# Token halves of the projections inside the k-tile loop: wh·xh0, wh·xl0, wh·xl1, wh·xh1, wl·xh1, wl·xh0

## The chip, the cores and the metric

The kernel runs on one core of a Trainium2 chip. The metric is the device time of one execution in microseconds (us), the median over several runs. The core has five engines that run beside each other, each through its own instructions in order: PE (TensorE, the matmuls, with PEld for its weight loads), DVE (VectorE), ACT (ScalarE), POOL (GpSimd) and SP (which issues DMAs here). They wait for each other by semaphores.

## The reference, cut to what matters

One layer of a decoder with two groups of heads side by side, 16 heads of stick-breaking attention ("sb") and 16 of sliding-window attention ("sw", 4 key and value heads), for 1024 tokens and a model width of 2048, in float32:

```python
h = rmsnorm(x, norm_pre)
proj = h @ w_in                    # (1024, 2048) @ (2048, 6656)
q_sb, k_sb, v_sb, z_sb, q_sw, k_sw, v_sw, z_sw = split(proj)
o_sb = stick_breaking_attention(q_sb, k_sb, v_sb)
o_sw = sliding_window_gqa(q_sw, k_sw, v_sw, sinks, rel_bias)
# each group: rmsnorm with its gain, times silu of its gate z
y = concat(gated o_sb, gated o_sw) @ w_out
out = x + rmsnorm(y, norm_post)
```

The change is in `h @ w_in`. The kernel computes it transposed: 52 row blocks of 128 output channels, each 128 x 1024 tokens.

## The kernel before

**The work.** x and the weights are each split into a high and a low part (xh and xl, whi and wlo), and a product is the sum of three matmuls: whi·xh, whi·xl and wlo·xh. From 0 to 76.7 us, x is loaded and split while three row blocks are computed. From 76.7 to about 1500 us the other 49 row blocks follow in the order of the list `work` (L727 to L735), one call of `proj` each. From 1500 us on comes the output projection (L909).

**One projection.** `proj` takes two PSUM tiles from `pproj` (L82), one for each half of the tokens (half 0 and half 1, 512 columns each). The tag has three buffers, and they rotate: half 0 of the next projection gets the buffer that is longest free, and half 1 of the next projection gets the buffer that half 0 of this one used. The depth of 2048 is 16 k-tiles of 128, in four weight groups `kg` of four. For each group `split_w` (L128) loads the weights, ACT makes whi (L133) and DVE makes wlo (L135); the split of the group after it is called at the head of each group. Within a group, the four k-tiles of half 0 come first, then those of half 1, three matmuls of 128 x 512 each: 96 matmuls for a projection.

**What is inserted.** After every three matmuls, `step()` (L252) may insert one piece of the attention, by a count of the PE time that the matmuls so far stand for: four matmuls z (the scores; then ACT's sigmoids L532 and L534, two scans on DVE L545 or L542, and a product L548), up to four transposes (wt, L126; then ACT's copy L563 and DVE's difference L564), or four matmuls o. Matmuls and transposes stay in program order on PE (L122, L126). The order of the other engines' instructions is set by a scheduler when the program is built.

**After a projection.** `proj` returns, and `done(ps)` in the main loop evacuates it: `scaled` (L362) multiplies a PSUM half with the row scale rstd on DVE (L366, 128 x 512, out of PSUM into a tile u), half 0 first. `evac_qk` splits and stores the result, `evac_v` transposes it, and `evac_z` gates the attention output with it (sigmoid L417, products L418 and L424). A half's PSUM buffer is free once L366 has read it.

Of the kernel before, what the change touches and what calls it, by code (L numbers as in the profile page):

```python
# [22 lines left out]
KT = D // P  # L23
HALF = 512
# [33 lines left out]
def layer(ctx, tc, xT, x, w_first, w_blk, w_out, g_pre, g_post, g_sb, g_sw, sinks, rel, onehot, penalty, out):  # L58
# [23 lines left out]
    def pproj(name):  # L82
        return ptile("pp", name, 3)
# [33 lines left out]
    def mm(ps, a, b, start, stop):  # L117
        n = 1
        for d in b.shape[1:]:
            n *= d  # L120
        pe_time[0] += n / 2400.0 * (4 if n < 256 or b.dtype == F32 else 1)
        tc.keep_in_program_order(nc.tensor.matmul(ps, a, b, start=start, stop=stop))  # L122
# [5 lines left out]
    def split_w(name, src):  # L128
        n = src.shape[1]
        raw = wr.tile([P, n, P], F32, tag="wraw", name=f"wraw_{name}", bufs=3)  # L130
        nc.sync.dma_start(raw, src)
        hi = wr.tile([P, n, P], F32R, tag="whi", name=f"whi_{name}")
        nc.scalar.copy(hi, raw)  # L133
        lo = wr.tile([P, n, P], F32R, tag="wlo", name=f"wlo_{name}")
        nc.vector.tensor_sub(lo, raw, hi.bitcast(F32))  # L135
        return hi, lo
# [15 lines left out]
    def advance(force=False):  # L152
        now = pe_time[0]
        while waiting and (force or waiting[0][0] <= now):
            todo.extend(waiting.pop(0)[1])
            prep()
        if later and (force or later[0][0] <= now):
            later.pop(0)[1]()
            return True
        if stage2 and (force or stage2[0][0] + stage2[0][1]["lag2"] <= now):  # L160
            u = stage2.pop(0)[1]
            u["s3"]()
            left[u["key"]] -= 1
            return True
        if stage1 and len(stage2) < 3 and (force or stage1[0][0] + stage1[0][1]["lag"] <= now):
            u = stage1.pop(0)[1]
            u["s2"]()
            stage2.append((pe_time[0], u))
            return True
        if todo and len(stage1) < todo[0]["depth"] and (force or last_start[0] + todo[0]["period"] <= now):  # L170
            u = todo.pop(0)
            if not u["ready"]:
                u["prep"]()
            last_start[0] = max(last_start[0] + u["period"], now - u["period"])
            u["s1"]()
            stage1.append((pe_time[0], u))
            prep()
            return True
        return False
# [10 lines left out]
    def background(force=False):  # L190
        for ch in chains:
            while force or pe_time[0] >= ch["at"]:
                if ch["job"] is None:
                    if not jobs:
                        break
                    ch["job"] = jobs.pop(0)(ch["buf"])
                wait = next(ch["job"], None)
                if wait is None:
                    ch["job"] = None
                else:  # L200
                    ch["at"] = pe_time[0] + wait
# [50 lines left out]
    def step():  # L252
        advance()
        background()
# [12 lines left out]
    xh, xl, xraw = [], [], []  # L267
# [73 lines left out]
    for k in range(KT):  # L341
# [11 lines left out]
        wh, wl = first.pop(0)  # L353
        parts = [(b, h) for h in range(2) for b in range(len(FIRST))]
        for b, h in sorted(parts) if k == KT - 1 else parts:
            for i, (wt, xt) in enumerate(((wh, xh[k]), (wh, xl[k]), (wl, xh[k]))):
                mm(ps0[b][h], wt[:, b, :], xt[:, h * HALF:(h + 1) * HALF],
                   start=(k == 0 and i == 0), stop=(k == KT - 1 and i == 2))
# [91 lines left out]
    def proj(b, name, nxt=None, mid=None):  # L450
        def get(b, name, kg):
            return split_w(f"{name}_{kg}", w_blk[b, :, 4 * kg:4 * kg + 4, :])

        if not splits:
            splits.append(get(b, name, 0))
        ps = [pproj(f"p_{name}_{h}") for h in range(2)]
        for kg in range(4):
            wh, wl = splits.pop(0)
            if kg == 2 and mid is not None:
                mid()  # L460
            if kg < 3:
                splits.append(get(b, name, kg + 1))
            elif nxt is not None:
                splits.append(get(*nxt, 0))
            for h in range(2):
                for j in range(4):
                    k = 4 * kg + j
                    for i, (wt, xt) in enumerate(((wh, xh[k]), (wh, xl[k]), (wl, xh[k]))):
                        mm(ps[h], wt[:, j, :], xt[:, h * HALF:(h + 1) * HALF],
                           start=(k == 0 and i == 0), stop=(k == KT - 1 and i == 2))  # L470
                    step()
        return ps

    kk = []
# [351 lines left out]
    for n, (b, name, done) in enumerate(work):  # L826
        nxt = work[n + 1][:2] if n + 1 < len(work) else None
        if DBG:
            print(name, f"{pe_time[0]:.0f}", {k: v for k, v in left.items() if v})
        ps = proj(b, name, nxt, mids.get(name))  # L830
        if n == len(work) - 3:
            drain(f"sb{NPAIR - 1}")
        if nxt is None:
            split_wo(2)
        done(ps)
        if n == len(work) - 3:
            open_ph2()
# [9 lines left out]
    def bank(name):  # L847
        tg = PT2[next(slots) % 8]
        return ptile(tg, name, PB[tg])
# [63 lines left out]
    for i in range(LAST + 1):  # L913
        nxt, src = [], []
        for dc in range(2):
            k0 = (2 * i + dc) * 8
            if i == LAST and dc == 1:
                split_wo(k0 + 8)
                for tb in range(4):
                    for h in range(1 + (tb == 3)):  # L920
                        part = slice(h * 256, (h + 1) * 256) if tb == 3 else whole
                        ps = bank(f"y{i}_{dc}_{tb}_{h}")[:, :part.stop - part.start]
# [8 lines left out]
            for e in range(8):  # L931
# [16 lines left out]
                if i == 5:  # L948
                    n = dc * 8 + e
                    residual("2", *pieces[n], scales[pieces[n][0]], x_rows[n])  # L950
                    load_row(n + 2)
                if i == LAST and dc == 0:
                    tb, h = divmod(e, 2)
# [58 lines left out]
```

## Time and profile before

| | |
|---|---|
| time, median of 3 runs | 1822.48 us (1818.33 to 1823.29) |
| profiled execution | 1825.41 us, its span 1823.7 us |
| busy share of PE, PEld, DVE, ACT, POOL | 98%, 82%, 68%, 43%, 27% |
| matmuls on record (weight loads as many) | 9046 |
| longest wait of PE after the first 20 us | 2.4 us (y for wohl, L775) |
| mean granted clock | 0.996 |

PE is the time in which a matmul is on the array, and PEld that of the weight loads beside it. The stretches named in the prediction are counted from the start of the span. Names in a row read out<-in: p_ is a projection's PSUM tile (its matmuls), u_ the evacuated half, whi_ and wlo_ the weight parts, z_, m_, b_, wt_, wh_, wl_ and o_ the tiles of an attention unit, in that order.

### The profile page before, as it was taken

The page shows a single profiled execution, that of the slowest core. Times are in us where ns is not written, and L with a number is a line of the kernel's source. Part 1 is how long each engine was busy: PE and PEld are TensorE (multiplying, and loading weights), DVE is VectorE, ACT ScalarE, POOL GpSimd, SP SyncE. Part 2 cuts the span into 40 slices and gives each one's busy share as a digit, 9 for nine tenths or more (in the row PEclk, how much of TensorE's full clock was granted, in tenths as well). Part 3 has the DMA queues.
Part 4 walks back from the last instruction along what each step waited for, and adds up shares of the span by engine and source line. Part 5 has one row for each costly group of instructions (what it writes and reads, how often), then busy time and mean ns, then how long its engine had stood idle before and what let it go on. Part 6 is the DMA issues. An engine that isn't in the chain of part 4 may idle for free. (4 is left out here: it accounts for less than half of the span.)

```text
span 1823.7 us, 27416 instructions
## 1 busy us (share of the span) xinstructions
PE 1786.3 (98%) x9046; PEld 1493.2 (82%) x9046; DVE 1242.3 (68%) x1984; ACT 787.2 (43%) x1696; POOL 496.2 (27%) x648
## 2 busy tenths in 40 slices
PE   8999999999999999999999999999999999999997
PEld 7788778887888888888888888888888877888886
DVE  7558842588557688587676787767868546745876
ACT  7345531355334344343443444434434434445432
POOL 0011121111213234133232332223303214504523
PEclk9999999999999999999999999999999999999999
DMA  7547775576746656466556563454524376533485
GB/s 229 193 143 206 197 202 167 163 205 199 217 145 191 179 159 199 138 191 173 174 163 181 159 183 124 135 176 127 175 76 132 116 227 211 189 107 128 145 248 184
DMA packets 205421, 312.50 MB, mean 171 GB/s; under 512 B 26176, under 2 KB 85728, under 8 KB 205152
## 3 DMA queue, kind: packets, MB, share of 16 engines
q1 hardware_dynamic: 203216, 307.61, 56.1%
q10 hardware_dynamic: 2064, 3.15, 0.5%
q8 instruction: 72, 1.18, 0.3%
q14 instruction: 69, 0.57, 0.1%
HBM read 219.42 MB, written 91.23 MB: 170 GB/s over the span
## 5 line engine op out<-in xcount | busy, mean ns | idle before, releaser
L545 DVE TENSOR_TENSOR_SCAN m_sb<-m_sb,m_sb,zero 128x257 f32<-128x257 f32 x192 | 159.9, 871 | 49.9 <-ACT m_sb L532 46.8
L548 DVE TENSOR_TENSOR b_sb<-b_sb,m_sb 128x512 f32<-128x512 f32 x160 | 128.3, 802 | 25.2 <-POOL b_sb L538 13.8
L532 ACT ACTIVATE m_sb<-z_sb 128x512 f32<-128x512 f32 x160 | 95.9, 600 | 114.4 <-PE z_sb L122 101.6
L542 DVE TENSOR_TENSOR_SCAN m_sb<-m_sb,mask 128x256 f32<-128x256 f32 x128 | 119.0, 967 | 38.6 <-ACT m_sb L532 36.9
L909 PE MATMUL y<-wohi,x 128*128 128x512 f32 x448 | 140.7, 390 | 0.5 <-ACT wohi L774 0.5
L563 ACT CAST wh_sb<-wt_sb 128x512 fp32r<-128x512 f32 (+1 forms) x160 | 87.0, 544 | 116.3 <-PE wt_sb L126 115.9
L909 PE MATMUL y<-wohl,x 128*128 128x512 f32 x576 | 134.4, 393 | 2.4 <-DVE wohl L775 2.4
L564 DVE TENSOR_TENSOR wl_sb<-wt_sb,wh_sb 128x512 fp32r<-128x512 f32 (+1 forms) x160 | 100.5, 631 | 45.4 <-ACT wh_sb L563 44.6
L909 PEld LDWEIGHTS y<-wohl,x 128*128 128x128 f32 x576 | 109.2, 190 | 25.7 <-DVE wohl L775 2.9
L122 PE MATMUL p_zsb<-xh,whi_zsb 128*128 128x512 f32 x256 | 103.9, 406 | 1.6 <-ACT whi_zsb L133 1.4
L122 PE MATMUL p_zsw<-xh,whi_zsw 128*128 128x512 f32 x256 | 104.8, 409 | 0.0
L122 PE MATMUL p_qsb<-xh,whi_qsb 128*128 128x512 f32 x256 | 104.5, 408 | 0.0
L122 PE MATMUL p_ksb<-xh,whi_ksb 128*128 128x512 f32 x256 | 104.4, 408 | 0.0
L122 PE MATMUL p_vsb<-xh,whi_vsb 128*128 128x512 f32 x256 | 102.9, 402 | 0.0
L122 PE MATMUL p_zsb<-xh,wlo_zsb 128*128 128x512 f32 x256 | 101.4, 396 | 1.3 <-DVE wlo_zsb L135 1.3
L122 PE MATMUL p_zsw<-xh,wlo_zsw 128*128 128x512 f32 x256 | 101.4, 396 | 0.0
L122 PE MATMUL p_zsw<-xl,whi_zsw 128*128 128x512 f32 x256 | 101.1, 395 | 0.0
L122 PE MATMUL p_ksb<-xh,wlo_ksb 128*128 128x512 f32 x256 | 101.1, 395 | 0.0
L122 PE MATMUL p_zsb<-xl,whi_zsb 128*128 128x512 f32 x256 | 101.1, 395 | 0.0
L122 PE MATMUL p_qsb<-xh,wlo_qsb 128*128 128x512 f32 x256 | 100.8, 394 | 0.0
L122 PE MATMUL p_ksb<-xl,whi_ksb 128*128 128x512 f32 x256 | 100.8, 394 | 0.0
L122 PE MATMUL p_vsb<-xh,wlo_vsb 128*128 128x512 f32 x256 | 100.6, 393 | 0.0
(242 smaller groups left out, 4926.7 us busy)
## 6 DMA issues: line engine op xcount, KB each, us to landing
row_sw<-in_w_out SPq DMA_DIRECT2D x80, 256.0 KB, 4.3
bg<-in_w_out SPq DMA_DIRECT2D x80, 256.0 KB, 4.2
woraw<-wsum SPq DMA_DIRECT2D x80, 256.0 KB, 3.4
kh<-kd SPq DMA_DIRECT2D x160, 64.0 KB, 3.0
kl<-kd SPq DMA_DIRECT2D x160, 64.0 KB, 2.8
wsum<-row_sw SPq DMA_DIRECT2D x40, 256.0 KB, 2.6
wsum<-bg SPq DMA_DIRECT2D x40, 256.0 KB, 2.8
q_sw<-qd SPq DMA_DIRECT2D x64, 128.0 KB, 3.4
```

The costliest lines, as they stand in the source:

```text
L122: tc.keep_in_program_order(nc.tensor.matmul(ps, a, b, start=start, stop=stop))
L532: nc.scalar.activation(m[:, :, 1:257], z, AF.Sigmoid, scale=-SCALE)
L542: nc.vector.tensor_tensor_scan(m[:, tb, 1:257], m[:, tb, 1:257], mask[:, P - P * tb:P - P * tb + 256], m[:, tb, 0:1], ALU.mult, ALU.max)
L545: nc.vector.tensor_tensor_scan(m[:, tb, :], m[:, tb, :], zero.to_broadcast([P, 257]), prev[:, tb, 256:257], ALU.mult, ALU.max)
L548: nc.vector.tensor_mul(beta, beta, m[:, :, 0:256])
L563: nc.scalar.copy(wh[:, :k], pt[:, :k])
L564: nc.vector.tensor_sub(wl[:, :k], pt[:, :k], wh[:, :k].bitcast(F32))
L909: nc.tensor.matmul(ps, xt[:, a, tcols], w[b][:, cols], start=first and n == 0, stop=last and n == 2)
```

## The change

The loop over the four k-tiles of a group becomes the outer one, and each k-tile takes its six matmuls for both halves in one go: wh·xh half 0, wh·xl half 0, wh·xl half 1, wh·xh half 1, wl·xh half 1, wl·xh half 0. The weights change twice in these six instead of four times. `step()` stays after every three matmuls. In the changed file the lines behind this place have numbers one higher.

```diff
-            for h in range(2):
-                for j in range(4):
-                    k = 4 * kg + j
-                    for i, (wt, xt) in enumerate(((wh, xh[k]), (wh, xl[k]), (wl, xh[k]))):
-                        mm(ps[h], wt[:, j, :], xt[:, h * HALF:(h + 1) * HALF],
-                           start=(k == 0 and i == 0), stop=(k == KT - 1 and i == 2))
-                    step()
+            for j in range(4):
+                k = 4 * kg + j
+                for n, (wt, xt, h) in enumerate(((wh, xh[k], 0), (wh, xl[k], 0), (wh, xl[k], 1),
+                                                 (wh, xh[k], 1), (wl, xh[k], 1), (wl, xh[k], 0))):
+                    mm(ps[h], wt[:, j, :], xt[:, h * HALF:(h + 1) * HALF],
+                       start=(k == 0 and n in (0, 2)), stop=(k == KT - 1 and n > 3))
+                    if n % 3 == 2:
+                        step()
```

What moves is seen best where one projection ends and the next begins. PE's order before, at the end of zsw3 and the start of qsb3 (`p_zsw3_1` is the PSUM tile of half 1 of zsw3, `xh15` the high part of k-tile 15; the last number of a name only counts tiles; a wait is named after the engine or DMA queue waited for):

```order
L122 MATMUL p_zsw3_1_7158<-xh15_692,whi_zsw3_3_7342 128x512
L122 MATMUL p_zsw3_1_7158<-xl15_693,whi_zsw3_3_7342 128x512
L122 MATMUL p_zsw3_1_7158<-xh15_692,wlo_zsw3_3_7344 128x512
L122 MATMUL p_qsb3_0_7520<-xh0_231,whi_qsb3_0_7420 128x512
L122 MATMUL p_qsb3_0_7520<-xl0_232,whi_qsb3_0_7420 128x512
L122 MATMUL p_qsb3_0_7520<-xh0_231,wlo_qsb3_0_7422 128x512
L122 MATMUL p_qsb3_0_7520<-xh1_239,whi_qsb3_0_7420 128x512
```

Half 1 ends the projection and half 0 begins the next one, and none of these matmuls waits for anything. PE's order now, at the same place:

```order
L122 MATMUL p_zsw3_1_7158<-xh15_692,whi_zsw3_3_7342 128x512
L122 MATMUL p_zsw3_1_7158<-xh15_692,wlo_zsw3_3_7344 128x512
L122 MATMUL p_zsw3_0_7157<-xh15_692,wlo_zsw3_3_7344 128x512
L122 MATMUL p_qsb3_0_7520<-xh0_231,whi_qsb3_0_7420 128x512
L122 MATMUL p_qsb3_0_7520<-xl0_232,whi_qsb3_0_7420 128x512
L122 MATMUL p_qsb3_1_7521<-xl0_232,whi_qsb3_0_7420 128x512 [waits DVE_49]
L122 MATMUL p_qsb3_1_7521<-xh0_231,whi_qsb3_0_7420 128x512
L122 MATMUL p_qsb3_1_7521<-xh0_231,wlo_qsb3_0_7422 128x512
L122 MATMUL p_qsb3_0_7520<-xh0_231,wlo_qsb3_0_7422 128x512
```

The last matmul of zsw3 goes to half 0, and the third matmul of qsb3 goes to half 1, whose buffer is that of zsw3's half 0; it waits for DVE, which reads that half at L366. A third matmul with this wait stands at each of the 48 boundaries between two projections of the list. In 8 of them four z matmuls lie between the last matmul and the third of the next projection, in 8 four o matmuls, and in some of the first 14 (up to 510 us) transposes.

DVE's order before, at the same boundary (SCALAR_TENSOR_TENSOR at L545 is what the profile calls TENSOR_TENSOR_SCAN):

```order
L366 TENSOR_TENSOR u_zsw3_0_7503<-p_zsw3_0_7157,rstd_209 128x512 [waits DMAHW3_49,PE_49]
L548 TENSOR_TENSOR b_sb1_1_0_0_7445<-b_sb1_1_0_0_7445,m_sb1_1_0_0_7443 128x512 [waits DVE_49,Pool_49]
L564 TENSOR_TENSOR wl_sb1_0_3_3_7467<-wt_sb1_0_3_3_7462,wh_sb1_0_3_3_7466 128x384 [waits Activation_49]
L418 SCALAR_TENSOR_TENSOR u_zsw3_0_7503<-u_zsw3_0_7503,gsw_198,sg_zsw3_0_7505 128x512 [waits Activation_49]
L424 TENSOR_TENSOR u_zsw3_0_7503<-u_zsw3_0_7503,or_zsw3_0_7337 128x512 [waits DMAHW7_49,DVE_49]
L366 TENSOR_TENSOR u_zsw3_1_7508<-p_zsw3_1_7158,rstd_209 128x512 [waits DMAHW2_49,PE_49]
L545 SCALAR_TENSOR_TENSOR m_sb1_1_0_1_7492<-m_sb1_1_0_1_7492,m_sb1_1_0_0_7443,zero_204 128x257 [waits Activation_49]
L545 SCALAR_TENSOR_TENSOR m_sb1_1_0_1_7492<-m_sb1_1_0_1_7492,m_sb1_1_0_0_7443,zero_204 128x257
```

And now:

```order
L549 TENSOR_TENSOR b_sb1_1_0_0_7445<-b_sb1_1_0_0_7445,m_sb1_1_0_0_7443 128x512 [waits DVE_49,Pool_49]
L565 TENSOR_TENSOR wl_sb1_0_3_3_7467<-wt_sb1_0_3_3_7462,wh_sb1_0_3_3_7466 128x384 [waits Activation_49]
L546 SCALAR_TENSOR_TENSOR m_sb1_1_0_1_7492<-m_sb1_1_0_1_7492,m_sb1_1_0_0_7443,zero_204 128x257 [waits Activation_49]
L546 SCALAR_TENSOR_TENSOR m_sb1_1_0_1_7492<-m_sb1_1_0_1_7492,m_sb1_1_0_0_7443,zero_204 128x257
L366 TENSOR_TENSOR u_zsw3_0_7503<-p_zsw3_0_7157,rstd_209 128x512 [waits DMAHW5_49,PE_49]
L549 TENSOR_TENSOR b_sb1_1_0_1_7494<-b_sb1_1_0_1_7494,m_sb1_1_0_1_7492 128x512 [waits DVE_49,Activation_49]
L366 TENSOR_TENSOR u_zsw3_1_7508<-p_zsw3_1_7158,rstd_209 128x512 [waits DMAHW4_49]
```

Half 0's evacuation stood ahead of the two scans of the unit that was inserted last, and stands behind them now. It is so at 8 of the 48 boundaries.

## Prediction

> **What bounds the kernel now.** I read the page's busy times first, then the busy time by stage, then the waits of TensorE, then single boundaries in the timeline. The windows below give, for the projections with the early attention units and for those with the later ones: length, then busy time and instructions of PE, PEld, DVE, ACT and POOL, the granted clock, the DMA share and GB/s.
>
> ```profile
> span 1823.7 us, 27416 instructions
> 76.70:510.00 433.30, 424.34 (x2193) 352.25 (x2192) 268.32 (x676) 178.27 (x546) 84.73 (x67) 1.00 0.65 188
> 510.00:1470.00 960.00, 954.58 (x5082) 808.41 (x5082) 689.02 (x936) 418.55 (x794) 282.15 (x484) 1.00 0.53 157
> ```
>
> TensorE is the bound: it is idle 9.0 us of the first stage and 5.4 us of the second, at full clock. DVE is busy 62% and 72% there, so it has room on the average, but what matters is when its one instruction comes that PE wants. Any wait added to PE in these 1393 us lengthens the run by nearly its own length, because there are only 14 us of idle time that it could replace. The profiled execution took 1825.41 us, 1.7 us more than its span and 2.9 us more than the median of the three runs, 1822.48; I work out a difference and add it to both.
>
> The quiet rhythm, columns start and duration in us, from a place where only projections run:
>
> ```profile
> 300.07 0.39 PE L122 MATMUL p_qsw<-xh,whi_qsw 128*128 128x512 f32 x1
> 300.07 0.19 PEld L122 LDWEIGHTS p_qsw<-xl,whi_qsw 128*128 128x128 f32 x1
> ...
> 302.79 0.39 PE L122 MATMUL p_qsw<-xh,whi_qsw 128*128 128x512 f32 x1
> ```
>
> Twelve starts lie 2.72 us apart, 0.227 us each (the 0.39 overlap). While the first matmul with whi runs, a weight load of the same whi for the next one is on record, although nothing changed; it lasts 0.19 and hides under a matmul of 0.227.
>
> **What the change does to a boundary.** Before, half 0 of a projection is complete 12 matmuls before its end, and half 1 of the next one, which takes half 0's buffer, starts 12 matmuls after it. Between the two lie 24 × 0.227 = 5.4 us for the evacuation on DVE. Now half 0 gets its last matmul as the very last of the projection, and the third matmul of the next one already writes into half 0's buffer, so 2 × 0.227 = 0.45 us are left. That happens at 48 boundaries (49 projections in the list). No matmul, load or split is added or removed, and the weight loads and splits stay at the head of their groups, so SP's and ACT's rows for them keep their place.
>
> **Price of a boundary where DVE is free (V, 9 of them).** After a v_sb projection nothing is inserted and no scan stands ahead. Matmuls and evacuation there now:
>
> ```profile
> 747.97 0.39 PE L122 MATMUL p_vsb<-xh,wlo_vsb 128*128 128x512 f32 x1
> ...
> 748.39 0.69 DVE L366 TENSOR_TENSOR u_vsb<-p_vsb,rstd 128x512 f32<-128x512 f32 x1 [2.54 <-PE p_vsb L122]
> ...
> 748.65 0.39 PE L122 MATMUL p_ksb<-xh,wlo_ksb 128*128 128x512 f32 x1
> ```
>
> The evacuation begins when the last matmul ends (748.36) and is through at 749.08; the third matmul of the next projection, free at 748.65, would start about 0.05 later, at 749.13. That is 0.48. How a wait on DVE ends and what the restart costs:
>
> ```profile
> 701.93 0.68 DVE L564 TENSOR_TENSOR wl_sb<-wt_sb,wh_sb 128x512 fp32r<-128x512 f32 x1
> ...
> 702.67 0.38 PE L122 MATMUL o_sb<-wl_sb,v_vsb 128*128 128x256 f32 x1 [1.14 <-DVE wl_sb L564]
> 702.89 0.28 PE L122 MATMUL o_sb<-wh_sb,v_vsb 128*128 128x256 f32 x1
> 703.01 0.28 PE L122 MATMUL o_sb<-wl_sb,v_vsb 128*128 128x256 f32 x1
> ```
>
> DVE ended at 702.61, PE started 0.06 later, and the first matmul after the wait held the array 0.22 where the next took 0.12: another 0.10. So 0.48 + 0.10, about 0.6, and 9 × 0.6 = 5.4 us.
>
> **Boundaries where DVE's order puts scans ahead (N, 8).** There the attention unit's z was inserted three matmuls before the end, and in the changed order the two scans that need ACT's sigmoid of z stand ahead of half 0's evacuation. At such a place (zsw3 to qsb3) the trace of before has the last z matmul, the last of zsw3, the third of qsb3, the sigmoid and the scans:
>
> ```profile
> 688.76 0.28 PE L122 MATMUL z_sb<-kl,q_sb 128*128 128x256 f32 x1
> ...
> 689.35 0.40 PE L122 MATMUL p_zsw<-xh,wlo_zsw 128*128 128x512 f32 x1
> ...
> 690.04 0.39 PE L122 MATMUL p_qsb<-xh,wlo_qsb 128*128 128x512 f32 x1
> ...
> 690.45 0.58 ACT L532 ACTIVATE m_sb<-z_sb 128x512 f32<-128x512 f32 x1
> ...
> 691.07 2.05 DVE L545 TENSOR_TENSOR_SCAN m_sb<-m_sb,m_sb,zero 128x257 f32<-128x257 f32 x2
> L545 DVE TENSOR_TENSOR_SCAN m_sb<-m_sb,m_sb,zero 128x257 f32<-128x257 f32 x192 | 159.9, 871 | 49.9 <-ACT m_sb L532 46.8
> ```
>
> If ACT takes z as soon as it is there (688.76 + 0.28), the sigmoid ends at 689.65; two mean scans (2 × 0.871) end at 691.4, the evacuation of 0.69 at 692.1. Against 690.04 that is 2.1. The first term is optimistic (ACT took z 1.4 us later here), the scans pessimistic (they include waiting for operands), so I take 1.9 plus the restart, 2.0: 8 × 2.0 = 16.0, with 1.6 and 2.5 as ends.
>
> **Boundaries with four matmuls inserted (Z and O, 16).** Four z or o matmuls of 0.12 lie between end and third matmul: 0.48, just what a free DVE needs. The cost is zero where DVE is free and up to about 0.9 where a 0.7 us copy is in its way; I take 0.3: 16 × 0.3 = 4.8. **The last one** (zsb6 to zsb7), behind splits on DVE, has no like row; I charge it as N, 2.0.
>
> **The early stage (14).** DVE also serves the sliding-window units. The instance at the end of a q_sb projection:
>
> ```profile
> 424.61 0.50 PE L122 MATMUL p_ksb<-xh,wlo_ksb 128*128 128x512 f32 x1
> ...
> 426.35 0.69 DVE L366 TENSOR_TENSOR u_qsb<-p_qsb,rstd 128x512 f32<-128x512 f32 x1
> ```
>
> The evacuation of half 1, at the end as half 0's will be, ended at 427.04, 2.5 us behind the free third matmul, since a softmax step stood ahead. I take two of 2.5 and twelve like V or a little more, 0.67: 5.0 + 8.0 = 13.0. The ends are 7 and 20.
>
> Sum of the added waits: 5.4 + 16.0 + 4.8 + 2.0 + 13.0 = 41.2 us.
>
> **What comes off.** PE's own waits (total, times, longest) that a later PE would no longer meet:
>
> ```profile
> PE wt_sw L126 <- DVE L_sw L631: 3.7, 5, 1.2
> ...
> PE p_zsb L122 <- ACT whi_zsb L133: 1.4, 1, 1.4
> PE p_zsb L122 <- DVE wlo_zsb L135: 1.3, 2, 0.7
> ```
>
> These 6.4 us go into the new waits at most once each; I take all. Then the kept weights. Per six matmuls, four instead of two are now followed by the same weights: 2/6 of 4704 = 1568 matmuls. In busy stretches (min/median/max, ns) the matmul that is followed by its own weights is the shorter by the median:
>
> ```profile
> L122 PE MATMUL p_qsb<-xh,whi_qsb x256: 387/390/504, 197.4 to 1244.1; 128*128 128x512 f32 x128
> ...
> L122 PE MATMUL p_qsb<-xh,wlo_qsb x256: 388/393/502, 198.1 to 1244.6; 128*128 128x512 f32 x128
> ```
>
> 1568 × 3 ns = 4.7 us less. The bounds are nothing (the quiet rhythm is the same with and without a change of weights) and the whole fixed part of a matmul: 2 × 0.12 for two of 256 columns against 0.227 for 512 leaves 13 ns, 1568 × 13 = 20 us. The Trainium skill (TensorE: Matmul & The Clock Gate, "Step-by-step: what each phase is for") says that weights can be loaded once and used for many matmuls, which speaks for this change; the trace has a load per matmul even where they stay, hidden, so I see nothing more to win from it.
>
> **The clock.** Three stretches, columns as in the windows above:
>
> ```profile
> 86.00:89.40 3.40, 2.23 (x12) 1.52 (x10) 1.69 (x3) 1.69 (x4) 0.10 (x1) 1.00 0.57 156
> 666.20:669.60 3.40, 1.43 (x8) 0.89 (x7) 3.30 (x3) 1.13 (x3) 3.40 (x4) 1.00 0.73 190
> 669.60:673.05 3.45, 3.45 (x12) 2.87 (x12) 3.35 (x6) 0.59 (x1) 0.48 (x3) 0.51 0.92 277
> ```
>
> A stretch with 1.97 us of idle time is followed by one at clock 0.51, which loses about 0.49 × 3.45 = 1.7 us; 1.17 us of idle brought none. Of the eleven long waits (8 N, 2 early, the last) a few will fall whole into one such stretch; I take +4, with 0 and 11 × 1.7 = 19 as ends.
>
> Net: 41.2 − 6.4 − 4.7 + 4 = +34. The profiled execution would be 1859.5, and the median 1856.5.
>
> **Rivals.** (a) *DVE is quicker than its order.* The scans end early and the inserted matmuls cover the rest: V 4.5, N 8 × 1.6 = 12.8, Z and O 0, early 7, last 2, together 26, less 6.4 and 4.7: +15, 1837. For it: DVE is idle 28 to 38% of the time. Against: its order is fixed, with scans ahead of the evacuation.
>
> (b) *Faster.* Weights that stay free the whole 13 ns, 20 us over the projections, and only the 26 boundaries with nothing inserted and no long queue pay, at 0.48: 12.5, less the 6.4: 1822.5 − 20 + 6 = 1808.5. It decides from about 7.5 ns saved per kept matmul on (6.1 us left of waits and the 5.5 of the bound below, over 1568). Against it stand the loads on record for unchanged weights and the same 0.227 with and without.
>
> (c) *Nothing much changes*: the same 20 us gain against the +26 of (a), less 6.4: 1822.
>
> (d) *The clock falls at every boundary.* 48 × 1.7 = 82 instead of 4: 1935. The Trainium skill (the same page, "A second HAM failure mode: psum-queue depth-cycling") describes short idle times of PE between groups, as PSUM buffers are cycled, that make the clock go down and up. The row with 1.17 us of idle time at full clock speaks against this for waits of 0.6.
>
> **Numbers.** My forecast, 1842 to 1876 with all ends mixed, 0.70, at its centre 1856; (a), 1830 to 1842, 0.16; (b) 0.05; (c) 0.04; (d) or a sum of all upper ends (N 2.5, Z and O 0.9, early 20, clock 19) 0.05. The range that holds 8 in 10 is 1834 to 1878. About 0.3%, 5.5 us, is what a measurement of this kernel can tell from no change: faster 0.05, within it 0.04, slower 0.91.
>
> **What the changed profile would show.** Right: PE waits on p_… for DVE u_… at L366, some 48 of them and 35 to 45 us in all, the longest at zsw and ksb projections with a scan just ahead on DVE; the same 9046 loads; the waits for L_sw and for zsb7's weights smaller. Wrong: that row with under 20 us (DVE came in time), a rhythm under 0.224 between kept matmuls (weights paid), fewer LDWEIGHTS than MATMULs, or many stretches with a clock of 0.5.

## The result and the profile after

The changed kernel takes 1873.67 us (median of 5 runs, 1869.37 to 1878.0) against 1823.29 us of the kernel before (5 runs). The ratio is 1.0278, 95% interval [1.0253, 1.0304]: about 50 us slower. Ratios are taken over the executions in the fast state; one of the six of the kernel with zsb7 early, below, took 6339.15 us, which counts in its median of 1834.78 and not in its ratio. The profiled execution took 1878.0 us, 52.6 more than that of before.

The page's busy times and the busy time by stage of the changed kernel (length; PE, PEld, DVE, ACT, POOL with instructions; clock; DMA share; GB/s):

```profile
PE 1804.8 (96%) x9046; PEld 1499.2 (80%) x9046; DVE 1245.9 (66%) x1984; ACT 792.6 (42%) x1696; POOL 497.7 (27%) x648
76.70:510.00 433.30, 413.42 (x2115) 344.10 (x2114) 262.21 (x672) 177.96 (x543) 80.37 (x62) 0.98 0.62 179
510.00:1470.00 960.00, 933.49 (x4925) 781.01 (x4925) 668.82 (x904) 406.18 (x764) 274.16 (x475) 1.00 0.52 154
```

The same matmuls and the same weight loads are on record, but in equal stretches of time there are fewer of them: 2115 instead of 2193, and 4925 instead of 5082. PE is now idle 19.9 and 26.5 us there. It was 9.0 and 5.4. What it waits for (total, times, longest):

```profile
PE z_sw L122 <- DMA q_sw<-qd: 8.6, 3, 4.2
...
PE p_zsw L122 <- DVE u_ksb L366: 5.6, 4, 1.8
PE p_zsb L122 <- DVE u_zsb L366: 4.7, 3, 2.7
PE o_sb L122 <- DVE wl_sb L565: 4.6, 6, 2.7
...
PE p_ksb L122 <- DVE u_qsb L366: 3.2, 3, 1.9
...
PE p_qsb L122 <- DVE u_ksw L366: 2.5, 1, 2.5
...
PE wt_sw L126 <- DVE L_sw L632: 0.6, 1, 0.6
...
PE p_ksb L122 <- DVE u_vsb L366: 0.3, 1, 0.3
```

Two kinds of wait are new, but for a single one of 0.2 us for u before. Sixteen rows of this view are waits of a projection's matmul for the evacuation u at L366, 33 waits with 30.5 us of idle time in all (the last row above is one of the smallest). And the row on top, which the prediction did not have: attention scores waiting for a load of q. The wait for L_sw has shrunk from 3.7 to 0.6 us, and those of zsb7's weights are gone. The wait of the o matmuls for wl_sb has grown, from 2.4 us in two waits to 4.6 in six.

One of the eight boundaries with scans (zsw3 to qsb3) in the changed kernel's timeline:

```profile
710.54 1.40 DVE L546 TENSOR_TENSOR_SCAN m_sb<-m_sb,m_sb,zero 128x257 f32<-128x257 f32 x2 [1.09 <-ACT m_sb L533]
710.58 0.40 PE L122 MATMUL p_qsb<-xl,whi_qsb 128*128 128x512 f32 x1
...
711.86 0.66 DVE L366 TENSOR_TENSOR u_zsw<-p_zsw,rstd 128x512 f32<-128x512 f32 x1
...
712.58 0.50 PE L122 MATMUL p_qsb<-xl,whi_qsb 128*128 128x512 f32 x1 [1.60 <-DVE u_zsw L366]
712.92 0.39 PE L122 MATMUL p_qsb<-xh,whi_qsb 128*128 128x512 f32 x1
```

The second matmul of qsb3 starts at 710.58, and the third could follow 0.227 later. It starts at 712.58, when the two scans and then the evacuation are through: 1.77 late. The next one follows after 0.34 instead of 0.23, so the boundary costs 1.88. The profile books only 1.60 of it as idle, because it counts from the modelled end of a matmul of 0.40, not from the rhythm of 0.227. A boundary behind a v_sb projection, where DVE is free:

```profile
649.69 0.39 PE L122 MATMUL p_zsw<-xl,whi_zsw 128*128 128x512 f32 x1
...
650.41 0.50 PE L122 MATMUL p_zsw<-xl,whi_zsw 128*128 128x512 f32 x1 [0.33 <-DVE u_vsb L366]
650.74 0.39 PE L122 MATMUL p_zsw<-xh,whi_zsw 128*128 128x512 f32 x1
```

Here 650.41 is 0.49 behind 649.69 + 0.227, and the restart adds 0.10. As an estimate from these two places, each of the 33 waits cost about 0.16 for the way of counting and 0.11 for the restart more than its row says: 30.5 + 33 × 0.27 = 39.4 us.

The mean granted clock of before, of the changed kernel and of its second profile, in that order, each from the cores' view of its run:

```profile
core 0: 1823.7 us, clock 0.996
```

```profile
core 0: 1876.3 us, clock 0.989
```

```profile
core 0: 1867.7 us, clock 0.992
```

A span times what its clock lacks from 1 is an estimate of the time that the lower clock cost: 7.3 us before, then 20.6 and 14.9. The clock is given to 0.001, so each of these can be off by 0.9 us.

### The profile page after: what moved, and what is told of

It reads as the page before. It is cut to its first block, busy times and chain, and to the rows that moved or that the text cites. A ratio compares the mean times of both kernels' runs of the same rounds, so it can differ in the third digit from the quotient of the medians.

```text
span 1876.3 us, 27417 instructions
## 1 busy us (share of the span) xinstructions
PE 1804.8 (96%) x9046; PEld 1499.2 (80%) x9046; DVE 1245.9 (66%) x1984; ACT 792.6 (42%) x1696; POOL 497.7 (27%) x648
## 5 line engine op out<-in xcount | busy, mean ns | idle before, releaser
L549 DVE TENSOR_TENSOR b_sb<-b_sb,m_sb 128x512 f32<-128x512 f32 x160 | 130.8, 817 | 26.7 <-POOL b_sb L539 10.5
L910 PEld LDWEIGHTS y<-wohl,x 128*128 128x128 f32 x576 | 110.1, 191 | 26.5 <-DVE wohl L776 3.4
L910 PEld LDWEIGHTS y<-wohi,x 128*128 128x128 f32 x448 | 84.1, 188 | 20.1 <-ACT wohi L775 2.6
L626 ACT ACTIVATE L_sw<-L_sw,nm_sw 128x256 f32<-128x256 f32 (+1 forms) x128 | 62.8, 491 | 79.5 <-DVE nm_sw L621 78.2
L535 ACT ACTIVATE b_sb<-z_sb 128x512 f32<-128x512 f32 x160 | 95.3, 596 | 0.0
L227 POOL TENSOR_TENSOR bg<-bg 128x512 f32<-128x512 f32 x40 | 57.2, 1430 | 141.0 <-DMA bg<-in_w_out 140.9
L126 PEld LDWEIGHTS wt_sb<-ident,b_sb 128*128 128x128 f32 x576 | 72.8, 141 | 24.0 <-PE p_qsb L122 1.4
L122 PE MATMUL p_zsb<-xl,whi_zsb 128*128 128x512 f32 x256 | 82.2, 398 | 9.2 <-DVE u_zsb L366 4.7
L910 PE MATMUL y<-wolo,x 128*128 128x512 f32 x224 | 87.6, 391 | 3.4 <-DVE wolo L776 3.4
L122 PE MATMUL p_zsw<-xl,whi_zsw 128*128 128x512 f32 x256 | 82.7, 399 | 8.5 <-DVE u_ksb L366 5.6
```

What stands on the lines that cost most here:

```text
L126: tc.keep_in_program_order(nc.tensor.transpose(ps, a, ident))
L227: BG((nc.gpsimd.tensor_add if sign > 0 else nc.gpsimd.tensor_sub)(t[:, 0, :], t[:, 0, :], t[:, 1, :]))
L535: nc.scalar.activation(beta, z, AF.Sigmoid, scale=SCALE)
L549: nc.vector.tensor_mul(beta, beta, m[:, :, 0:256])
L626: nc.scalar.activation(L[:, hh, :n], L[:, hh, :n], AF.Exp, bias=nm[:, hh:hh + 1], accum_out=sm[:, hh:hh + 1])
L910: nc.tensor.matmul(ps, xt[:, a, tcols], w[b][:, cols], start=first and n == 0, stop=last and n == 2)
```

## The experiments

The ratios below are to the kernel before as it was measured beside each run; its medians there were 1817 to 1818 us, so times in us are best compared by these ratios.

The theory: all of the loss comes from half 0 being complete only at the end of a projection. It makes PE wait at the boundaries, longest where DVE's order has scans ahead, and it makes others wait who read half 0. Kept weights are worth nothing. The rivals: the new order of six matmuls costs by itself; the waits are the unavoidable way through DVE; kept weights are worth 3 ns or more.

**The last weight group in the old order.** The `if` chooses the old loop for one group:

```diff
+            if kg == 3:
+                for h in range(2):
+                    for j in range(4):
+                        ...
+            else:
                 for j in range(4):
```

> The last weight group of each projection in the old order (half 0's twelve matmuls, then half 1's), the other three groups in the new one. Theory: the loss is all from half 0 being complete only at the end; here it is complete 12 matmuls before, so PE waits for no evacuation and the loads of q for the sliding window come in time: 1823 us, as before. If weights that are kept are worth 3 ns each, 1176 more of them give 3.5 us: 1819.5; at 13 ns 15 us: 1808. Rival: the six-matmul order itself costs (reading x in another order, alternating PSUM tiles), so three quarters of the loss stay: about 1861.

Measured: 1820.0 us, ratio 1.0003 [0.999, 1.0015]. The waits for q are gone, and two for u are left, of 1.4 and 0.6 us. The whole loss is gone although three quarters of the matmuls are in the new order, so that order itself costs nothing. It brings nothing either: 3 ns for each of the 1176 more matmuls with kept weights would have been a ratio of 0.9981, outside the interval. The two waits left for u cost some 2.5 us with the corrections above and could hide most of such a gain; the kernel with the weights back, below, does not have this weakness.

**The first weight group in the old order** (the same edit with `kg == 0`).

> The first weight group of each projection in the old order, the other three in the new one: half 0 is still complete only at the end, but half 1 of the next projection starts 12 matmuls later. Theory: the waits for the evacuation (31 us, and some of the stretches at half clock after them) are gone, and what stays is what a late half 0 does to others than PE's buffers: the loads of q for the sliding window, two waits of 4.3 us, and the three or four stretches at half clock around them (1.7 us each): 1832 to 1838. Rival: those DMA waits came from PE's own delay and go with it: 1823. Rival: the six-matmul order costs: about 1861.

Measured: 1833.55 us, 1.0091 [1.0075, 1.0106]. No wait for u is left, but the wait for q is:

```profile
PE z_sw L122 <- DMA q_sw<-qd: 6.8, 2, 3.5
```

So PE's waits at the boundaries, with the half clock after them, are worth 1.028/1.0091, 1.9% or 34 us, and a late half 0 costs 0.9% (16.5 us) in another way. That is a little more than expected (1838 against 1823 is 0.8%); the wait for q is not all of it.

**The evacuation ahead in DVE's order.**

```diff
-        if scale is None:
+        with tc.high_priority(HURRY):
+            if scale is None:
```

> The changed kernel, with the evacuation of the halves given a higher priority for DVE's order; at the boundaries with scans only the first of the two scans still stands ahead. Theory: those eight waits fall from 1.8 to about 1.0 us, the others stay (0.5 where DVE is free): 6 to 7 us less, and 1.7 for each stretch at half clock that goes: 1864 to 1868. Rival: the waits are the way from the last matmul through DVE and back and not the queue on DVE: no change, 1874.

Measured: 1864.81 us, 1.0251 [1.0235, 1.0268]. The boundary from zsw3 to qsb3:

```profile
702.87 0.75 DVE L547 TENSOR_TENSOR_SCAN m_sb<-m_sb,m_sb,zero 128x257 f32<-128x257 f32 x1 [1.09 <-ACT m_sb L534]
703.54 1.26 DVE L367 TENSOR_TENSOR u_zsw<-p_zsw,rstd 128x512 f32<-128x512 f32 x2
```

```profile
704.26 0.50 PE L122 MATMUL p_qsb<-xl,whi_qsb 128*128 128x512 f32 x1 [0.95 <-DVE u_zsw L367]
```

With one scan ahead instead of two, the wait is 0.95 instead of 1.60, and all waits for u of this profile come to 23.9 us instead of 30.5 and 28.5 in the two profiles of the changed kernel. The trace shows the theory's size. The intervals of the two ratios overlap, so the time alone would not, and that it lies between 1864 and 1868 us says little, since every kernel was a few us faster in these runs.

**Weights back, halves as they are.**

```diff
-((wh, xh[k], 0), (wh, xl[k], 0), (wh, xl[k], 1), (wh, xh[k], 1), (wl, xh[k], 1), (wl, xh[k], 0))
+((wh, xh[k], 0), (wl, xh[k], 0), (wh, xl[k], 1), (wh, xh[k], 1), (wl, xh[k], 1), (wh, xl[k], 0))
```

> The changed kernel, with the weights in the order hi, lo, hi, hi, lo, hi within a k-tile, the halves as they were: two of six matmuls are followed by their own weights, as before the change, instead of four. Theory (kept weights are worth nothing): 1874, and the same 0.229 to 0.231 us from matmul to matmul. Rival: 3 ns for each of 1568, 4.7 us more: 1878.5; 13 ns each: 1894.

Measured: 1863.86 us, 1.0255 [1.0241, 1.0269]. Not slower, so the rival with a price on kept weights fails. It fails by more than the expectation says: in this order only one of six matmuls (the third) is followed by its own weights, not two, so three of six differ from the changed kernel, 2352 in all, which at 3 ns would be 7.1 us. It came out somewhat below the changed kernel, which none had said; the intervals overlap, and the cause stays open. The matmuls of q_sb with xl and whi before, then two rows of the changed kernel (min/median/max in ns):

```profile
L122 PE MATMUL p_qsb<-xl,whi_qsb x256: 387/393/398, 197.7 to 1244.4; 128*128 128x512 f32 x128
```

```profile
L122 PE MATMUL p_qsb<-xh,whi_qsb x256: 387/390/628, 203.6 to 1287.0; 128*128 128x512 f32 x128
...
L122 PE MATMUL p_qsb<-xl,whi_qsb x256: 387/393/796, 203.9 to 1286.8; 128*128 128x512 f32 x128
```

The row of xl with whi, which never kept its weights before and always does now, has the 393 that it had. So the 3 ns go with the pair xh and whi and not with keeping; why they do is not shown.

**Who else waits for half 0.** Three kernels on the base of the one with the first group in the old order (no waits at the boundaries), with half 0 early for some projections only:

```diff
-            if kg == 0:
+            if kg == 0 or (kg == 3 and name.startswith("qsw")):                    # q
+            if kg == 0 or (kg == 3 and nxt is None):                               # zsb7
+            if kg == 0 or (kg == 3 and name.startswith(("qsw", "zsw", "zsb"))):    # q and z
```

> As the kernel whose first weight group is in the old order, and in the projections of the sliding-window q the last group too, so that their half 0 is complete 12 matmuls before the end. Theory: of the 0.91% that a late half 0 still costs without PE's buffer waits, the two waits of z_sw for the load of q (6.8 us) and the stretches at half clock right after them (3.4 us) go: 1.0035 to 1.0055 of the time before. Rival: z_sw waits for something else (the order of SP's queue at large): no change, 1.009.

Measured: 1828.2 us, 1.006 [1.0042, 1.0078]; no wait for q is left. The ratio is a little above what was expected (up to 1.0055), which its interval still holds. The interval just touches that of the base; the trace settles it.

> As the kernel whose first weight group is in the old order, and in the last projection (zsb7) the last group too. Theory: the output projection starts late because ACT and DVE have both halves of zsb7 and the first output weights to do at once; with half 0 early its wait for wohi (3.4 us, and a stretch at half clock of 1.7) goes: 1.006 to 1.007 of the time before. Rival: that wait varies from run to run and has nothing to do with it: 1.009.

Measured: 1834.78 us, 1.0097 [1.0072, 1.0122]. No gain; the wait for wohi at the start of the output projection is still there:

```profile
PE y L919 <- ACT wohi L784: 3.2, 1, 3.2
```

So it is not the last projection that makes this wait, and that idea fell. In SP's queue of this kernel, around that place, the load of the output weights (woraw) stands behind five loads b of gated outputs:

```profile
1497.87 2.38 SPq L865 DMA_DIRECT2D b<-ogd  x5
1500.47 0.45 SPq L765 DMA_DIRECT2D woraw<-wsum  x1
```

That suggested the z projections ahead of the last one, whose gated outputs these are. It only suggests it: in the kernel before, too, five loads b (from 1492.50 us) stand ahead of a load woraw (1495.95).

> The first weight group of each projection in the old order, and the last group too in the projections of the sliding-window q and of both z; the half 0 of the other q, k and v is still complete at the end. Theory: the 0.6% that are left with the q alone come from the late half 0 of z (its gating and the transfers behind it are late, up to the first weights of the output projection): 1.000 to 1.002. Rival: from the k, v and the other q, or from two evacuations back to back on DVE in general: 1.006.

Measured: 1819.51 us, 1.0016 [1.0, 1.0031], apart from the 1.006 of q alone. The rest of the 0.9% was the late half 0 of z; with q and z early, the other q, k and v may be late at no cost that can be told from nothing. Which z, and through which transfer in each case, was not tried.

**One k-tile by halves.** In the first and last k-tile (then in one of them), half 0 gets its three matmuls first:

```diff
+                if k in (0, KT - 1):      # then: k == KT - 1, and k == 0
+                    six = six[:2] + six[5:] + six[2:5]
```

> The changed kernel, but in the first and the last k-tile of a projection half 0 has its three matmuls and then half 1: between the last matmul of half 0 and the first of the next half 1 lie 6 matmuls instead of 2, 0.9 us more. Theory: every wait at a boundary falls by 0.9 us or to nothing: none where DVE is free, 0.9 instead of 1.8 where scans stand ahead, 2.0 instead of 2.9 twice: 20 us less than the changed kernel, 1.016 to 1.018 of the time before. Rival: the wait depends on what DVE does, which comes later by as much: 1.025.

Measured: 1826.02 us, 1.0045 [1.0028, 1.0061], far better than either theory said. The scheduler had put the evacuation ahead of the scans at all eight boundaries, which the expectation did not reckon with. The next two kernels separate that from the time between.

> The changed kernel, but in the last k-tile of a projection half 0 has its three matmuls first: half 0 is complete 3 matmuls before the end, 5 ahead of the first matmul of the next half 1 instead of 2 (0.68 us more). In DVE's order the evacuation of half 0 then stands ahead of the two scans at all eight boundaries where it stood behind them. Theory: it is this order that makes the long waits; they go, and with them those of 0.5: 1.004 to 1.008 of the time before. Rival: only the time between counts; each wait gets 0.68 shorter, 1.1 us stay at the eight: 1.014 to 1.018.

> The changed kernel, but in the first k-tile of a projection half 0 has its three matmuls first: half 0 is still complete only at the end, half 1 starts one matmul later (0.23 us), and the scans still stand ahead of the evacuation at eight boundaries. Theory: waits of 1.8 become 1.55 and those of 0.5 become 0.26, some 8 us less of all: 1.022 to 1.025 of the time before, far from the kernel with the last k-tile by halves, though the two edits look alike. Rival (any room at the boundary frees it): 1.005 to 1.01.

Measured: 1829.87 us, 1.007 [1.0053, 1.0086], with the last k-tile by halves, and 1855.07 us, 1.0211 [1.0192, 1.0231], with the first. The boundary from zsw3 to qsb3, first with the last k-tile by halves, then with the first:

```profile
687.43 0.69 DVE L366 TENSOR_TENSOR u_zsw<-p_zsw,rstd 128x512 f32<-128x512 f32 x1
...
688.59 1.40 DVE L549 TENSOR_TENSOR_SCAN m_sb<-m_sb,m_sb,zero 128x257 f32<-128x257 f32 x2 [0.46 <-ACT m_sb L536]
688.62 0.63 PE L122 MATMUL p_qsb<-xl,whi_qsb 128*128 128x512 f32 x2
```

```profile
705.46 1.40 DVE L549 TENSOR_TENSOR_SCAN m_sb<-m_sb,m_sb,zero 128x257 f32<-128x257 f32 x2 [1.09 <-ACT m_sb L536]
...
706.78 0.66 DVE L366 TENSOR_TENSOR u_zsw<-p_zsw,rstd 128x512 f32<-128x512 f32 x1
...
707.50 0.50 PE L122 MATMUL p_qsb<-xl,whi_qsb 128*128 128x512 f32 x1 [1.37 <-DVE u_zsw L366]
```

In the first, the evacuation begins while the last matmuls of half 1 still run, the scans come after it, and PE goes on without a wait. So it is at six of the eight; behind ksb2 a wait of 0.44 is left, and behind ksb7 one of 1.66, where a product and a difference of the attention, ahead of the evacuation, come late. In the second, the scans stand ahead as in the changed kernel, and the wait is 1.37 instead of 1.60, less by just the one matmul of room. Three matmuls earlier for half 0 bring 2.1 of the 2.8%, one matmul later for half 1 brings 0.7. The 0.7 is rather more than the waits at the boundaries alone explain (0.23 for each), just below what was expected (1.022). Not all of the 2.1 comes from the boundaries either: that kernel still has 11 waits for u, 11.5 us in all, but its waits for q are 2.4 us, against 8.6 and 5.6 in the two profiles of the changed kernel. A half 0 that is three matmuls earlier thus seems to serve its other readers better, too.

**The changed kernel again**, on the chip of the others.

> The changed kernel once more, on the chip of the others: 1.0278 of the time before; by the kernel with the weights in the old order, 1.0255, every theory says the same of both if kept weights are worth nothing.

Measured: 1869.21 us, 1.028 [1.026, 1.03].

## Why the prediction was right, point by point

The time fell into the range, with the sign forecast, and the size was 50 us where the text had 34. That it still fell into the range is in part luck: the upper end had been drawn for longer boundaries and a lower clock, and it took in a loss on a path that the sum did not have.

**The boundaries** were sized rightly: 41.2 us forecast, 39.4 by the rows of the profile and the two corrections above. The N kind was put at 2.0 and is 1.88 in the row shown, V at 0.6 and is 0.59, the two long ones of the early stage at 2.5 and show idle times of 2.5 (u_ksw) and 1.9. By kind, with the 0.27 added to each wait of the first profile: V 5.5 us for 5.4 forecast, N 16.2 for 16.0, Z and O 4.5 for 4.8 (five waits of 0.62 and eleven of nothing), the last one 3.0 for 2.0, the early stage 10.5 for 13.0. So the sum is right term by term, with errors of 1 to 2.5 us of both signs in the last two. The mark set for being wrong, "under 20 us" of such waits, was not met, and the 35 to 45 us named as right were 30.5 as the profile counts. That scans ahead on DVE make the long ones is shown by the pair of kernels with one k-tile by halves, and by the one with the evacuation ahead. Rival (a), DVE quicker than its order, fails with them: the order held.

**What comes off**: the waits for L_sw and for zsb7's weights gave 3.1 and 2.7 us, 5.8 of the 6.4.

**The kept weights** were booked as 4.7 us less and are worth nothing. The 3 ns were read from two groups that differ in the x part as well as in what follows, and taken for the latter. With it fall rivals (b) and (c), which needed up to 13 ns. The sentence of the Trainium skill on loading weights once (TensorE: Matmul & The Clock Gate, "Step-by-step: what each phase is for") finds nothing here: the changed kernel has 9046 loads for 9046 matmuls, as before.

**The clock** was booked at 4 us and took 13.3 in the first profile and 7.6 in the second. Stretches of the first profile with a long wait and the stretches behind them, at the boundaries after zsw3, ksb2 and ksb7, and one stretch behind a wait for q of 4.17 us (columns as above):

```profile
709.00:712.60 3.60, 2.00 (x12) 1.39 (x10) 2.51 (x5) 1.70 (x5) 0.00 (x0) 1.00 0.52 144
712.60:716.00 3.40, 3.40 (x18) 2.91 (x19) 3.40 (x6) 2.12 (x4) 0.81 (x1) 1.00 0.00 0
587.00:590.40 3.40, 1.63 (x10) 1.06 (x8) 3.17 (x6) 1.68 (x4) 0.24 (x2) 1.00 0.65 200
590.70:594.00 3.30, 3.30 (x12) 2.77 (x11) 2.15 (x3) 0.86 (x2) 2.98 (x3) 0.54 0.81 219
1318.50:1322.20 3.70, 1.06 (x6) 0.54 (x4) 3.25 (x7) 1.60 (x4) 0.59 (x2) 1.00 0.14 35
1322.20:1325.70 3.50, 3.50 (x19) 2.96 (x20) 2.51 (x3) 1.59 (x4) 2.84 (x2) 1.00 0.41 149
417.00:423.60 6.60, 5.60 (x17) 4.74 (x18) 1.70 (x4) 1.47 (x5) 0.00 (x0) 0.50 0.28 86
```

The boundary after ksb7 in the second profile:

```profile
1308.50:1312.20 3.70, 1.27 (x6) 0.70 (x5) 3.60 (x6) 1.59 (x3) 0.23 (x2) 1.00 0.14 35
1312.20:1315.70 3.50, 3.26 (x8) 2.59 (x9) 2.75 (x4) 1.24 (x2) 2.58 (x2) 0.52 0.34 123
```

A wait of 1.6 left the clock at 1.00 at the first place; 1.77 us idle in 3.40 at the second was followed by 0.54. At the third, 2.64 us idle left it at 1.00, and the same boundary in the second profile, with 2.43 us idle in the stretch, was followed by 0.52. So the length of a wait does not decide alone, and not every boundary throttles: rival (d), 48 × 1.7 us, is six times the 13.3. Nor are the 13.3 us the price of the boundaries alone, since the clock fell behind waits for q as well. The Trainium skill's account of it (TensorE: Matmul & The Clock Gate, "A second HAM failure mode: psum-queue depth-cycling") agrees in kind, since the clock does go down behind some of these waits, and not in extent.

**The step that failed** is in the part on what the change does to a boundary: "the weight loads and splits stay at the head of their groups, so SP's and ACT's rows for them keep their place". That is so, and it was taken for all that SP does. The stores of the two halves, and the loads that read them back, were not followed. Before, half 0 of a q was stored (L376) 4.8 us ahead of half 1. Now both are stored in one go, and a load of q for sliding-window units falls back in SP's queue. Before:

```profile
160.96 0.39 SPq L376 DMA_DIRECT2D qd<-hi_qsw  x1
...
165.76 0.53 SPq L376 DMA_DIRECT2D qd<-hi_qsw  x1
...
168.14 0.59 SPq L224 DMA_DIRECT2D bg<-in_w_out  x1
168.78 0.45 SPq L225 DMA_DIRECT2D bg<-in_w_out  x1
169.33 1.25 SPq L605 DMA_DIRECT2D q_sw<-qd  x2
```

And now, with PE's side of it:

```profile
166.50 0.54 SPq L376 DMA_DIRECT2D qd<-hi_qsw  x1
...
167.60 0.39 SPq L376 DMA_DIRECT2D qd<-hi_qsw  x1
...
172.58 0.61 SPq L500 DMA_DIRECT2D od<-ot_sw  x1
173.29 0.54 SPq L601 DMA_DIRECT2D bias<-biasd  x1
173.93 1.25 SPq L606 DMA_DIRECT2D q_sw<-qd  x2
```

```profile
180.68 0.36 PE L122 MATMUL z_sw<-kh,q_sw 128*128 128x256 f32 x1 [4.15 <-DMA q_sw<-qd]
```

The load is issued 4.6 us later, behind the loads of the bias and other stores, and PE stands still for 4.15 us. With two more, the longer of 4.17, that is 8.6 us in the first profile. All that a late half 0 does besides PE's buffers is 0.9%, 16.5 us, by the kernel with the first group in the old order; that is as much as lies between 34 and 50. That the boundaries alone are worth 34 us there, just the net sum forecast, is partly chance: the 4.7 us taken off for kept weights have no ground, and the clock was booked too low.

So the terms between the two profiles are 39.4 − 5.8 + 13.3 + 8.6 = 55.5, for 52.6 measured. The other waits of the view do not close this: some are shorter (b_sb 3.0 before, 1.2 now), some longer (wl_sb 2.4 and 4.6), and together they add 1.5 us. So the terms are some 4 us too long in sum, and which of them is too long is not shown; the 0.27 for each wait and the clock are estimates.

## What to carry to other kernels

When a change makes a result complete later, follow each of its readers, not only the one whose buffer it holds: here a third of the loss came from late readers of half 0, for q through stores and loads in a queue that the diff does not touch, for z on a path that was not followed. How long a wait gets is set by what stands ahead of the evacuation on its engine, so a few matmuls of room can be worth far more than their own length, when they let a scheduler put it first: one k-tile by halves brought the 2.8% down to 0.7. Before paying for kept weights, look whether their loads are hidden; here each was, and the gain was nil.

## What the hardware showed that was not expected

A weight load stands on record for each matmul, also in a row of four with the same weights, and lasts 0.19 us under a matmul of 0.227. The clock fell to about half (0.54) behind a wait within a stretch of 3.4 us that held 1.77 us of idle time (587.0 to 590.4), and stayed full behind one with 1.60 (709.0 to 712.6) and behind one with 2.64 (1318.5 to 1322.2). The Trainium skill (TensorE: Matmul & The Clock Gate, "Why this matters for your kernels") warns of idle times above about 3 us; here little more than half of that was enough at one place. Since the order of DVE and SP is set when the program is built, moving half 0's last matmul three places ahead within one k-tile took away six of the eight waits behind scans (about 1.60 us each in the changed kernel's profile) and shortened the other two.
